# A first adaLN layer with half of one shift computed by columns on VectorE, loads in a fixed order, and sums of squares by tokens on ScalarE

## The chip, the cores and the metric

The kernel runs on one core of a Trainium2 chip. The metric is the device time of one execution in microseconds (us), the median of three runs. TensorE multiplies matrices, VectorE (DVE in the profile), ScalarE (ACT) and GpSimd (POOL) work element by element, and SyncE (SP) issues most of the transfers from the device's main memory (HBM).

## The reference: what is computed

Two layers over 1024 latent tokens and 256 context tokens of width 1024, all in fp32. Layer 0 mixes tokens by retention (4 heads), layer 1 by a short gated convolution; each is followed by a SwiGLU layer. Ahead of each mixer stands an RMS norm whose result is shifted and scaled (adaLN):

```python
def ada_params(cond, w, b):
    return jnp.split(jax.nn.silu(cond) @ w + b, 6, axis=-1)
def modulate(x, shift, scale):
    return x * (1 + scale) + shift
sh1, sc1, g1, sh2, sc2, g2 = ada_params(c, ada_w[i], ada_b[i])
ax = modulate(rms_norm(hx, norm_mix[i]), sh1, sc1)            # latent tokens
csh1, csc1, ... = ada_params(c_ctx, ada_w[i], ada_b[i])
ac = modulate(rms_norm(hc, norm_mix[i]), csh1, csc1)          # context tokens, layer 0
qx, kx, vx, gx = jnp.split(ax @ w_qkvg, [D, 2 * D, 4 * D], axis=-1)
kc, vc = jnp.split(ac @ w_qkvg[:, D:4 * D], [D], axis=-1)
```

Only the front of layer 0 matters here: the first shift (chunk 0 of the adaLN matrix, 1024 columns) and scale (chunk 1) for both conditions c and c_ctx, the norms of context and x, and the products of the context with the weights of k and v.

## The kernel before

Activations stand transposed: features on the 128 partitions (8 tiles, kt), tokens along the free axis. Every fp32 operand of a large product is split into a high and a low part of type fp32r (`split`, L132 on ScalarE and L133 on VectorE), and a product takes three passes of TensorE (`mm3`, L137 to L139).

The first adaLN is computed by `ada_both`, once for chunk 1 and once for chunk 0. For each half of 512 columns it loads four pieces of 512 KB (`ada_raw`, L169), multiplies them with the two columns Silu(c) and Silu(c_ctx) (`sc`) as the 2-column stationary operand (L237), copies the two result rows out of PSUM (L242), and turns them into columns by four small transposes (L247) into a bank `cps`; then it adds the bias (L252). The sixteen products of a half stand as 32 records in the trace, since each goes through TensorE in two passes. The later adaLN chunks are computed otherwise (`ada_next`, L210): VectorE multiplies a load of 128 transposed columns with a row Silu(c) that stands on all partitions (`c_row`, L192 and L193) and sums along the row in the same instruction.

The context tokens are loaded ahead of it (L489, on ScalarE's queue), squared on ScalarE (L261, L264), added on VectorE (L265), summed over features by products with ones (`rstd`, L270), and 1/rms is made on VectorE with small integer and float steps (L275, L143 to L155). 1/rms becomes diagonal matrices (L288), a product with ones spreads it over the partitions (`spread`, L296), and VectorE multiplies the context with scale and 1/rms (L512). With the shift added on the way (L527, L528) the context is the split operand `ac`.

Then `ctx_layer` multiplies the context with six blocks of weights, two of k and four of v. A block takes two loads of 1 MB (`ctx_load`, two pieces of 512 KB each, L483, from a pool of six such pieces), eight splits, and 96 records of L137 to L139 in two banks. Its two results are copied out at its end (L814) and stored. Between the products `unit_done` takes work from a queue of hooks: for each half of x (512 tokens) the squares (`sq`: ScalarE squares, GpSimd adds, L265), the diagonals (`diag`, with L270), the scaling (`mod`, L558 and L561), and the operands of the next products. x is loaded transposed, sixteen loads of 256 KB (`load_x`, L538).

The order of instructions on an engine, the SP queue with its loads included, is not that of the program: a list scheduler fills it with what is ready by its own estimate of time. That is how L483 loads stand ahead of the last four L169 loads, and the load of c_row ahead of x.

Of the kernel before, what the change touches and what calls it, by code (L numbers as in the profile page):

```python
# [52 lines left out]
def hybrid_kernel(ctx: ExitStack, tc: tile.TileContext, a: dict):  # L53
# [19 lines left out]
    def ttile():  # L73
        return tp.tile([P, 512], F32, tag="t", name="tt")
# [15 lines left out]
    def bank():  # L90
        return pp.tile([P, 512], F32, tag="p", name="ps")

    cols = const.tile([P, N_COLS], F32, name="cols")
    nc.sync.dma_start(cols, a["cols"])
    cc = const.tile([P, KT, 2], F32, name="cc")
    nc.sync.dma_start(cc, a["cc"])
    sc = const.tile([P, KT, 2], F32, name="sc")
# [66 lines left out]
    def ada_raw(b):  # L164

        out = []
        for half in range(2):
            r = raw()
            nc.sync.dma_start(r, a["ada_w"][b, :, half * 1024 : (half + 1) * 1024])  # L169
            out += [r[:, k * 256 : (k + 1) * 256] for k in range(4)]  # L170
        return out
# [19 lines left out]
    def ada_start():  # L191
        nc.sync.dma_start(c_row, a["c_row"].to_broadcast([P, D]))  # L192
        nc.scalar.activation(c_row, c_row, AF.Silu)  # L193
        ada_load(0)
        ada_load(1)
# [32 lines left out]

    def ada_both(i, chunk, mid=nothing):

        cps = bank()
        for half in range(2):
            ps = bank()
            for e in range(2):
                r = ada_raw(chunk * 4 + half * 2 + e)
                for kt in range(KT):
                    nc.tensor.matmul(  # L237
                        ps[:2, e * 256 : (e + 1) * 256], sc[:, kt], r[kt],
                        start=kt == 0, stop=kt == KT - 1,
                    )  # L240
            row = ttile()
            nc.scalar.copy(row[:2], ps[:2])  # L242
            if half == 0:
                mid()
# [5 lines left out]
        out = const.tile([P, KT, 2], F32, name=f"adab_{i}_{chunk}")  # L250
        o = C_ADAB + i * 48 + chunk * 8
        nc.vector.tensor_tensor(  # L252
            out, cps[:, : 2 * KT].rearrange("p (k v) -> p k v", v=2),
            cols[:, o : o + 8].unsqueeze(2).to_broadcast([P, KT, 2]), op=ALU.add,
        )
        return out


    def sq_add(acc, h, first, n=512, eng=nc.vector):
        if first:  # L260
            nc.scalar.activation(acc[:, :n], h, AF.Square)  # L261
        else:
            s = ttile()
            nc.scalar.activation(s[:, :n], h, AF.Square)  # L264
            eng.tensor_tensor(acc[:, :n], acc[:, :n], s[:, :n], op=ALU.add)  # L265

    def rstd(acc, nb, ps):

        for j in range(nb):
            nc.tensor.matmul(  # L270
                ps[:, j : j + 1], acc[:, j * P : (j + 1) * P], ones[:, 0:1],
                start=True, stop=True,
            )
        v = sm.tile([P, 8], F32, tag="rs_v", name="rs_v")
        nc.vector.tensor_scalar(  # L275
            v[:, :nb], ps[:, :nb], 1.0 / D, EPS, op0=ALU.mult, op1=ALU.add
        )
        y = sm.tile([P, 8], F32, tag="rs_y", name="rs_y")
        rsqrt(y[:, :nb], v[:, :nb], nb)
        return y  # L280

    def rstd_diag(acc, n):

        nb = n // P
        y = rstd(acc, nb, bank())
        dg = ttile()
        for j in range(nb):
            nc.vector.tensor_scalar(  # L288
                dg[:, j * P : (j + 1) * P], ident, y[:, j : j + 1], None, op0=ALU.mult
            )  # L290
        return dg

    def spread(dg, n):
# [183 lines left out]

    def piece(src):

        out = []  # L480
        for e in range(2):
            r = raw2()
            nc.sync.dma_start(r, src[:, e * 1024 : (e + 1) * 1024])  # L483
            out += [r[:, :512], r[:, 512:]]
        return out

    ct = [ttile() for _ in range(KT // 2)]
# [6 lines left out]
    box = {}  # L494
    s1 = ada_both(0, 1, lambda: box.update(dg=rstd_diag(acc, CTX)))
    to_scale(s1, cols[:, C_NMIX : C_NMIX + 8].unsqueeze(2).to_broadcast([P, KT, 2]))
# [4 lines left out]
    def ctx_load(n):  # L501
        if n < 2 * len(ctx_blocks):
            c_raws[n] = piece(ctx_blocks[n // 2][n % 2])

# [3 lines left out]

    def middle():
        rb = spread(box["dg"], CTX)  # L510
        for kt, h in enumerate(ch):
            nc.vector.scalar_tensor_tensor(  # L512
                h, h, s1[:, kt, 1:2], rb[:, :CTX], op0=ALU.mult, op1=ALU.mult
            )
        ctx_load(0)
        ctx_load(1)
        for kt in range(4):
            ctx_weight(0, kt)

    sh1 = ada_both(0, 0, middle)  # L520
    ac = {}
# [12 lines left out]
    xc = {n: {} for n in S_ALL}  # L534

    def load_x(tb):
        for kt in range(KT):
            nc.sync.dma_start(xt[kt, tb], a["xT"][kt, tb])  # L538

    def x_hooks(tb):  # L540
# [3 lines left out]
        def sq(k2):  # L544
            if k2 == 0:
                box["acc"] = ttile()
            for kt in (2 * k2, 2 * k2 + 1):
                sq_add(box["acc"], xt[kt, tb], kt == 0, TB, nc.gpsimd)

        def diag():  # L550
            box["dg"] = rstd_diag(box["acc"], TB)

# [1026 lines left out]
def _layout(i):  # L1579
# [13 lines left out]
    def paired(w):  # L1593
# [6 lines left out]
    arrays = {  # L1600
        "xT": i["x"][0].reshape(NTB, TB, KT, P).transpose(2, 0, 3, 1),
        "cxT": i["ctx"][0].reshape(CTX, KT // 2, 2, P).transpose(1, 3, 2, 0)
        .reshape(KT // 2, P, 2 * CTX),
# [4 lines left out]
        ),  # L1608
        "c_row": i["c"],
        "ada_w": i["ada_w"][0, :, : 2 * D].reshape(KT, P, -1, 256).transpose(2, 1, 0, 3)  # L1610
        .reshape(-1, P, KT * 256),
        "ada_t": np.concatenate([i["ada_w"][l, :, n * D : (n + 1) * D].T for l, n in ADA])
        .reshape(-1, P, D),
# [35 lines left out]
```

## Time and profile before

| | before |
|---|---|
| median of three runs | 2627.14 us (2623.88 to 2627.67) |
| profiled execution | 2628.3 us, its span 2626.4 us |
| TensorE busy (matmul) | 2565.5 us, 98% of the span |
| VectorE busy | 1889.3 us, 72% |
| ScalarE busy | 1235.6 us, 47% |
| GpSimd busy | 323.7 us, 12% |
| moved by DMA | 445.12 MB, mean 169 GB/s |

Times in rows are counted from the start of the span. A row of the timeline gives start, duration, engine, source line, operation, what it writes and reads, a count, and in brackets the idle time before it and what ended it. PE is TensorE, PEld its weight loads, SPq and ACTq are the sequencers that issue transfers. A row of a window gives the length, then the busy time of each engine with the number of instructions, the granted TensorE clock (1.00 is full speed), the DMA share and GB/s. A row of groups gives busy time and mean ns of one, then the idle time before them and what ended it.

### The profile page before, as it was taken

What the parts mean: (1) busy time and instruction counts of PE and PEld (TensorE: products, weight loads), DVE (VectorE), ACT (ScalarE), POOL (GpSimd) and SP (SyncE); (2) the same over time, 40 slices, a digit from 0 to 9 for tenths busy, and PEclk for the clock granted to TensorE, in tenths of its full rate; (3) what the DMA queues carried; (4) which work ended last, traced back from release to release, by engine and by line L of the source; (5) the groups of instructions that cost most, each with busy time, mean ns of one, the idle gap of its engine ahead of it and who ended that gap; (6) DMA issues with size and microseconds to landing.
All of it is one profiled execution on the core that took longest, in us unless ns stands there. A gap on an engine that the chain in (4) does not pass through costs nothing.

```text
span 2626.4 us, 33369 instructions
## 1 busy us (share of the span) xinstructions
PE 2565.5 (98%) x11508; PEld 2099.9 (80%) x11508; DVE 1889.3 (72%) x3333; ACT 1235.6 (47%) x2239; POOL 323.7 (12%) x370
## 2 busy tenths in 40 slices
PE   8999999999989999999999999999999999999998
PEld 4788888887777787888887888788777888887888
DVE  4886766767887867777776767777688666655766
ACT  4653232447776545433333545533366333333544
POOL 1100222002332102000001100200112000002100
PEclk9999999999999999999999999999999999999999
DMA  9546233764569957444556945432685333329733
GB/s 328 203 149 220 92 124 128 260 216 132 182 217 279 272 157 161 135 157 153 181 187 214 276 138 172 91 100 98 181 240 103 117 104 112 109 89 299 199 88 117
DMA packets 218985, 445.12 MB, mean 169 GB/s; under 512 B 23104, under 2 KB 52928, under 8 KB 218816
## 3 DMA queue, kind: packets, MB, share of 16 engines
q1 hardware_dynamic: 149232, 297.94, 35.4%
q0 software_dynamic: 32864, 79.19, 12.4%
q10 hardware_dynamic: 36720, 65.86, 6.7%
q8 instruction: 91, 1.49, 0.2%
q14 instruction: 78, 0.64, 0.1%
HBM read 320.74 MB, written 109.58 MB: 164 GB/s over the span
## 4 chain that ended last, share of the span: by engine, by line
PE 86%; DVE 6%; DMA 5%; issue 2%; ACT 1%; SPq 0%; DVEq 0%; ACTq 0%
PE ps L137 28%; PE ps L138 28%; PE ps L139 27%; DVE u L133 2%; PE ps L237 1%; DMA tt<-x_d 1%; DMA tt<-os_d 1%; DMA tt<-g_d 1%; DVE u L675 1%; PE ps L947 0%; DVE kh L634 0%; PE ps L296 0%; DMA raw<-in_w_g 0%; DVE tt L265 0%; PE ps L270 0%
## 5 line engine op out<-in xcount | busy, mean ns | idle before, releaser
L137 PE MATMUL ps<-u 128*128 128x512 f32 (+1 forms) x3492 | 1363.7, 391 | 17.9 <-DVE u L133 8.5
L138 PE MATMUL ps<-u 128*128 128x512 f32 (+1 forms) x3492 | 1356.7, 389 | 2.1 <-DVE u L133 1.9
L139 PE MATMUL ps<-u 128*128 128x512 f32 (+1 forms) x3492 | 1355.9, 389 | 0.0
L137 PEld LDWEIGHTS ps<-u 128*128 128x128 f32 x3492 | 659.1, 189 | 162.5 <-ACT u L132 10.0
L138 PEld LDWEIGHTS ps<-u 128*128 128x128 f32 x3492 | 659.7, 189 | 137.7 <-DVE u L133 4.7
L139 PEld LDWEIGHTS ps<-u 128*128 128x128 f32 x3492 | 659.4, 189 | 135.1 <-issue 0.7
L132 ACT CAST u<-raw 128x512 fp32r<-128x512 f32 x622 | 375.5, 619 | 379.9 <-PE ps L139 234.3
L133 DVE TENSOR_TENSOR u<-raw,u 128x512 fp32r<-128x512 f32 x622 | 434.8, 711 | 60.2 <-ACT u L132 59.4
L133 DVE TENSOR_TENSOR u<-tt,u 128x512 fp32r<-128x512 f32 x358 | 242.2, 700 | 123.4 <-ACT u L132 121.4
L132 ACT CAST u<-tt 128x512 fp32r<-128x512 f32 x358 | 211.9, 620 | 206.0 <-DMA tt<-x_d 102.4
L443 ACT COPY tt<-ps 128x512 f32<-128x512 f32 x192 | 112.6, 587 | 251.8 <-PE ps L139 244.5
L128 DVE SCALAR_TENSOR_TENSOR u<-raw,u 128x512 fp32r<-128x512 f32 x168 | 114.9, 688 | 76.6 <-ACT u L127 76.4
L127 ACT ACTIVATE u<-raw 128x512 fp32r<-128x512 f32 x168 | 105.1, 632 | 88.2 <-PE ps L139 75.8
L1263 POOL DMA_DIRECT2D x_d<-tt x52 | 28.3, 544 | 837.6 <-DVE tt L1276 774.2
L456 DVE TENSOR_TENSOR tt<-tt,ps 128x512 f32<-128x512 f32 x64 | 43.8, 684 | 80.3 <-PE ps L139 80.2
L675 DVE SCALAR_TENSOR_TENSOR u<-ps,u 128x512 fp32r<-128x512 f32 x128 | 84.9, 684 | 20.8 <-ACT u L674 20.7
L624 POOL TENSOR_TENSOR u<-t,u 128x512 fp32r<-128x512 f32 x40 | 55.3, 1386 | 279.3 <-ACT u L623 269.9
L450 DVE TENSOR_TENSOR tt<-tt,ps 128x512 f32<-128x512 f32 x64 | 44.0, 687 | 61.8 <-ACT tt L443 58.4
L674 ACT ACTIVATE u<-ps 128x512 fp32r<-128x512 f32 x128 | 74.2, 598 | 28.8 <-PE ps L139 26.8
L1146 DVE SCALAR_TENSOR_TENSOR t<-ps,ada,t 128x512 f32<-128x512 f32 x48 | 33.9, 747 | 53.3 <-PE ps L139 52.0
L210 DVE SCALAR_TENSOR_TENSOR raw<-raw,c_row 128x512 f32<-128x512 f32 x84 | 55.2, 686 | 20.1 <-DMA raw<-in_ada_t 20.0
L446 DVE TENSOR_TENSOR tt<-tt,ps 128x512 f32<-128x512 f32 x64 | 43.8, 684 | 23.7 <-PE ps L139 23.7
(162 smaller groups left out, 2054.5 us busy)
## 6 DMA issues: line engine op xcount, KB each, us to landing
tt<-x_d SPq DMA_DIRECT2D x182, 256.0 KB, 4.6
raw<-in_w SPq DMA_DIRECT2D x88, 512.0 KB, 4.1
raw<-in_w SPq DMA_DIRECT2D x88, 256.0 KB, 5.4
raw<-in_ada_t SPq DMA_DIRECT2D x42, 512.0 KB, 5.2
x_d<-tt ACTq DMA_DIRECT2D x78, 256.0 KB, 2.3
t<-in_ada_t SPq DMA_DIRECT2D x76, 256.0 KB, 6.3
raw<-in_w_v SPq DMA_DIRECT2D x36, 512.0 KB, 4.7
x_d<-tt POOLq DMA_DIRECT2D x52, 256.0 KB, 2.7
```

The lines of the kernel that those rows point to most:

```text
L127: nc.scalar.activation(dst_hi, src, AF.Copy, scale=-1.0)
L128: nc.vector.scalar_tensor_tensor(dst_lo, src, -1.0, dst_hi.bitcast(F32), op0=ALU.mult, op1=ALU.subtract)
L132: nc.scalar.copy(dst_hi, src)
L133: nc.vector.tensor_sub(dst_lo, src, dst_hi.bitcast(F32))
L137: nc.tensor.matmul(ps, w_hi, x_lo, start=first, stop=False, **kw)
L138: nc.tensor.matmul(ps, w_lo, x_hi, start=False, stop=False, **kw)
L139: nc.tensor.matmul(ps, w_hi, x_hi, start=False, stop=last, **kw)
L210: nc.vector.scalar_tensor_tensor(w[e], w[e], 1.0, c_row[:, k], op0=ALU.mult, op1=ALU.mult, accum_out=sums[:, e, ct : ct + 1],)
L443: nc.scalar.copy(m[p, n], ps)
L624: nc.gpsimd.tensor_sub(t[:, 1], v, t[:, 0].bitcast(F32))
L674: nc.scalar.activation(s[:, 0], st[d][m], AF.Copy, scale=f)
L675: nc.vector.scalar_tensor_tensor(s[:, 1], st[d][m], f, s[:, 0].bitcast(F32), op0=ALU.mult, op1=ALU.subtract,)
```

## The change

- The loads of the front and of the context products are pinned: `in_order` keeps them on the SP queue in the program's order, which is cc, four adaLN pieces of chunk 1, context, a column load, four of chunk 1, c_row, three column loads, four of chunk 0, and then context weights, x and rows of x. cols moves to ScalarE's queue.
- Half of chunk 0, the columns 512 to 1023, is no longer computed by TensorE. Four loads of 128 transposed columns (`ada_e`, 512 KB each) are multiplied on VectorE with the rows Silu(c) and Silu(c_ctx) and summed in the same instruction: 16 passes over 128x512, with c_ctx as soon as it can be, with c behind the scale. The row of c_ctx is loaded once (4 KB) and spread over the partitions by two products with ones; Silu is taken from PSUM. The row of c is loaded to all partitions as before, but earlier.
- The two half chunks of `ada_both` become `ada_half` with a `turn` that is called later.
- The sums of squares of x come from a second load of x, by tokens (`xr`, eight loads of 512 KB into the pool of split operands): ScalarE squares a tile of 128 tokens x 1024 features and sums along the row in the same instruction. The sums on GpSimd and the products of L270 for x fall away. The second half of x is loaded in the second block of the context products, the rows in the first.
- The hooks of x begin six empty steps later, and from the second block on two are taken at a time.

```diff
+    def in_order(dst, src):
+        tc.keep_in_program_order(nc.sync.dma_start(dst, src))
...
+    cx_row = raw()
+    nc.scalar.dma_start(cx_row[:1], a["cx_row"])
...
-    def ada_both(i, chunk, mid=nothing):
+    def ada_half(cps, chunk, half, between=nothing):
...
+    def early_load():
+        early_w.append(raw())
+        in_order(early_w[-1], a["ada_e"][len(early_w) - 1])
+
+    def early_sums(n, sums, v, out):
+        for e in range(2):
+            k = slice(e * 512, (e + 1) * 512)
+            nc.vector.scalar_tensor_tensor(
+                out, early_w[n][:, k], 1.0, (c_row, cx_row)[v][:, k], op0=ALU.mult, op1=ALU.mult,
+                accum_out=sums[:, e, n, v : v + 1],
+            )
...
+    for e in range(2):
+        k, ps = slice(e * 512, (e + 1) * 512), bank()
+        nc.tensor.matmul(ps, ones[:1], cx_row[:1, k], start=True, stop=True)
+        nc.scalar.activation(cx_row[:, k], ps, AF.Silu)
...
+    turn = ada_half(cps, 1, 0)
     ct = [ttile() for _ in range(KT // 2)]
     for t, src in zip(ct, a["cxT"]):
-        nc.scalar.dma_start(t, src)
+        in_order(t, src)
+    early_load()
...
+    early_sums(0, early, 1, junk)
+    dg = rstd_diag(acc, CTX)
+    turn()
+    turn = ada_half(cps, 1, 1)
+    in_order(c_row, a["c_row"].to_broadcast([P, D]))
+    nc.scalar.activation(c_row, c_row, AF.Silu)
+    for n in range(1, KT // 2):
+        early_load()
+        early_sums(n, early, 1, junk)
+    turn()
...
-    sh1 = ada_both(0, 0, middle)
+    cps = bank()
+    turn = ada_half(cps, 0, 0)
+    rb = spread(dg, CTX)
+    for kt, h in enumerate(ch):
+        nc.vector.scalar_tensor_tensor(
+            h, h, s1[:, kt, 1:2], rb[:, :CTX], op0=ALU.mult, op1=ALU.mult
+        )
+    for n in range(KT // 2):
+        early_sums(n, early, 0, junk)
...
+    ctx_load(0)
+    ctx_load(1)
+    turn()
...
+    def load_rows(tb):
+        for c in range(tb * 4, tb * 4 + 4):
+            xrows[c] = raw()
+            in_order(xrows[c], a["xr"][c])
...
         def sq(k2):
-            for kt in (2 * k2, 2 * k2 + 1):
-                sq_add(box["acc"], xt[kt, tb], kt == 0, TB, nc.gpsimd)
+            c = tb * 4 + k2
+            nc.scalar.activation(
+                xrows[c], xrows[c], AF.Square, accum_out=x_ss[:, c : c + 1]
+            )
...
         load_x(0)
         ctx_load(2)
-        load_x(1)
...
                     ctx_load(2 * b + 3 + kt // 4)
+                    if b == 0:
+                        load_rows(kt // 4)
+                    elif (b, kt) == (1, 0):
+                        load_x(1)
...
-                    unit_done(2 if b > 1 and kt % 4 == 1 else 1)
+                    unit_done(2 if b else 1)
...
-    hooks.extend(sq0 + mod0)
+    hooks.extend([nothing] * 6 + sq0 + mod0)
```

More of the change, by code (lines that the diff above doesn't have):

```diff
@@ L168, in ada_raw @@
             r = raw()
-            nc.sync.dma_start(r, a["ada_w"][b, :, half * 1024 : (half + 1) * 1024])
+            in_order(r, a["ada_w"][b, :, half * 1024 : (half + 1) * 1024])
             out += [r[:, k * 256 : (k + 1) * 256] for k in range(4)]
@@ L191, in ada_start @@
     def ada_start():
-        nc.sync.dma_start(c_row, a["c_row"].to_broadcast([P, D]))
-        nc.scalar.activation(c_row, c_row, AF.Silu)
         ada_load(0)
@@ L227, in urgent, with turn @@
         hooks.extendleft(reversed(work))
-    def ada_both(i, chunk, mid=nothing):
[L231 to L244, printed above, removed]
+    def ada_half(cps, chunk, half, between=nothing):
+        ps = bank()
+        raws = []
+        for e in range(2):
+            raws.append(ada_raw(chunk * 4 + half * 2 + e))
+            between()
+        for e, r in enumerate(raws):
+            for kt in range(KT):
+                nc.tensor.matmul(
+                    ps[:2, e * 256 : (e + 1) * 256], sc[:, kt], r[kt],
+                    start=kt == 0, stop=kt == KT - 1,
+                )
+        row = ttile()
+        nc.scalar.copy(row[:2], ps[:2])
+        def turn():
             for n in range(4):
@@ L249, in ada_both, with ada_bias @@
                 )
-        out = const.tile([P, KT, 2], F32, name=f"adab_{i}_{chunk}")
-        o = C_ADAB + i * 48 + chunk * 8
+        return turn
+    def ada_bias(out, src, chunk, c):
+        o = C_ADAB + chunk * 8
+        bias = cols[:, o + c.start : o + c.stop].unsqueeze(2)
         nc.vector.tensor_tensor(
-            out, cps[:, : 2 * KT].rearrange("p (k v) -> p k v", v=2),
-            cols[:, o : o + 8].unsqueeze(2).to_broadcast([P, KT, 2]), op=ALU.add,
-        )
-        return out
+            out[:, c], src, bias.to_broadcast([P, c.stop - c.start, 2]), op=ALU.add
+        )
+    early_w = []
+    def early_load():
[8 more added lines that the diff above has]
+            )
     def sq_add(acc, h, first, n=512, eng=nc.vector):
@@ L265, in sq_add, with root @@
             eng.tensor_tensor(acc[:, :n], acc[:, :n], s[:, :n], op=ALU.add)
+    def root(sums, nb):
+        v = sm.tile([P, 8], F32, tag="rs_v", name="rs_v")
+        nc.vector.tensor_scalar(
+            v[:, :nb], sums, 1.0 / D, EPS, op0=ALU.mult, op1=ALU.add
+        )
+        y = sm.tile([P, 8], F32, tag="rs_y", name="rs_y")
+        rsqrt(y[:, :nb], v[:, :nb], nb)
+        return y
     def rstd(acc, nb, ps):
@@ L273, in rstd, with diagonals @@
             )
[L274 to L285, printed above, removed]
+        return root(ps[:, :nb], nb)
+    def diagonals(y, n):
         dg = ttile()
-        for j in range(nb):
+        for j in range(n // P):
             nc.vector.tensor_scalar(
@@ L291, in rstd_diag @@
         return dg
+    def rstd_diag(acc, n):
+        return diagonals(rstd(acc, n // P, bank()), n)
     def spread(dg, n):
@@ L475, in hybrid_kernel, with piece @@
     h_d = spilled("h_d", KT, NTB)
-    def piece(src):
+    def piece(src, load=nc.sync.dma_start):
         out = []
@@ L482, in piece @@
             r = raw2()
-            nc.sync.dma_start(r, src[:, e * 1024 : (e + 1) * 1024])
+            load(r, src[:, e * 1024 : (e + 1) * 1024])
             out += [r[:, :512], r[:, 512:]]
         return out
+    for e in range(2):
+        k, ps = slice(e * 512, (e + 1) * 512), bank()
+        nc.tensor.matmul(ps, ones[:1], cx_row[:1, k], start=True, stop=True)
+        nc.scalar.activation(cx_row[:, k], ps, AF.Silu)
+    s1 = const.tile([P, KT, 2], F32, name="adab_0_1")
+    sh1 = const.tile([P, KT, 2], F32, name="adab_0_0")
+    early = sm.tile([P, 2, KT // 2, 2], F32, name="early", bufs=1)
+    junk = ttile()
+    cps = bank()
+    turn = ada_half(cps, 1, 0)
     ct = [ttile() for _ in range(KT // 2)]
     for t, src in zip(ct, a["cxT"]):
-        nc.scalar.dma_start(t, src)
+        in_order(t, src)
+    early_load()
     ch = [ct[kt // 2][:, (kt % 2) * CTX : (kt % 2 + 1) * CTX] for kt in range(KT)]
@@ L507, in ctx_weight @@
             c_ws[b, kt] = in_parts(c_raws[2 * b + kt // 4][kt % 4])
[L509 to L518, printed above, removed]
-    sh1 = ada_both(0, 0, middle)
+    cps = bank()
+    turn = ada_half(cps, 0, 0)
[3 more added lines that the diff above has]
+            h, h, s1[:, kt, 1:2], rb[:, :CTX], op0=ALU.mult, op1=ALU.mult
+        )
+    for n in range(KT // 2):
+        early_sums(n, early, 0, junk)
+    nc.vector.tensor_add(early[:, 0], early[:, 0], early[:, 1])
+    ada_bias(sh1, early[:, 0], 0, slice(KT // 2, KT))
+    ctx_load(0)
+    ctx_load(1)
+    turn()
+    ada_bias(sh1, cps[:, :KT].rearrange("p (k v) -> p k v", v=2), 0, slice(0, KT // 2))
+    for kt in range(4):
+        ctx_weight(0, kt)
     ac = {}
```

22 lines of the change are left out of this document (12 added, 10 removed).

## The prediction

> **What bounds the kernel now.** I read the page first, for the bound of the whole.
>
> ```profile
> span 2626.4 us, 33369 instructions
> PE 2565.5 (98%) x11508; PEld 2099.9 (80%) x11508; DVE 1889.3 (72%) x3333; ACT 1235.6 (47%) x2239; POOL 323.7 (12%) x370
> PE 86%; DVE 6%; DMA 5%; issue 2%; ACT 1%; SPq 0%; DVEq 0%; ACTq 0%
> ```
>
> TensorE sets the end. What the change can win is therefore time at the front, until TensorE begins the products of the first layer, and holes in the products just behind; from there on the same products follow one another, and I expect them only to shift. So I took the busy times by stage and the timeline of the first 44 us.
>
> ```profile
> core 0: us, PE busy (x) PEld busy (x) DVE busy (x) ACT busy (x) POOL busy (x), PEclk, DMA share, GB/s
> 9.00:43.40 34.40, 32.75 (x150) 12.99 (x148) 10.29 (x33) 6.30 (x14) 0.00 (x0) 1.00 1.03 402
> 43.40:58.00 14.60, 13.74 (x51) 10.48 (x52) 11.49 (x16) 14.60 (x31) 7.00 (x5) 0.88 0.70 238
> ```
> ```profile
> 1.66 16.08 SPq L169 DMA_DIRECT2D raw<-in_ada_w  x12
> 8.89 9.19 PE L237 MATMUL ps<-raw,sc 128*2 128x256 f32 x32 [8.89 <-DMA raw<-in_ada_w]
> 18.23 1.78 SPq L483 DMA_DIRECT2D raw<-in_w_kc  x4
> 19.14 7.93 PE L237 MATMUL ps<-raw,sc 128*2 128x256 f32 x36
> 20.22 4.14 SPq L169 DMA_DIRECT2D raw<-in_ada_w  x4
> 27.33 6.21 PE L237 MATMUL ps<-raw,sc 128*2 128x256 f32 x28
> 34.53 7.07 PE L237 MATMUL ps<-raw,sc 128*2 128x256 f32 x32
> 41.64 0.57 ACT L242 COPY tt<-ps 2x512 f32<-2x512 f32 x1 [7.49 <-PE ps L237]
> 43.48 0.86 PE L137 MATMUL ps<-u 128*128 128x512 f32 x2 [0.81 <-ACT u L527]
> ```
>
> The adaLN is four quarters of 32 records (32, 36, 28, 32 by the order in which they were put). TensorE waits 8.9 us for the first weights, is then busy nearly throughout, and the first context product starts at 43.5. The transfers are full as well (402 GB/s), but not all of that is needed: context weights (L483) pass the last four adaLN loads.
>
> Then the context products, 43.5 to 118:
>
> ```profile
> 43.40:47.10 3.70, 1.49 (x3) 0.96 (x4) 0.57 1.05 386
> 50.44 0.39 PE L139 MATMUL ps<-u 128*128 128x512 f32 x1
> 51.56 0.50 PE L137 MATMUL ps<-u 128*128 128x512 f32 x1 [0.73 <-DVE u L133]
> 62.92 0.95 PE L270 MATMUL ps<-ones,tt 128*128 128x1 f32 x8
> 71.80 0.39 PE L139 MATMUL ps<-u 128*128 128x512 f32 x1
> 74.09 1.50 PE L296 MATMUL ps<-tt,ones 128*128 128x512 f32 x2 [1.90 <-DVE tt L288]
> 75.60:78.20 2.60, 2.60 (x7) 2.02 (x7) 2.57 (x4) 1.79 (x3) 0.00 (x0) 0.53 1.04 401
> 84.43 1.27 ACT L814 COPY tt<-ps 128x512 f32<-128x512 f32 x2 [0.36 <-PE ps L139]
> 95.25 1.27 ACT L814 COPY tt<-ps 128x512 f32<-128x512 f32 x2 [0.20 <-PE ps L139]
> 118.02 1.27 ACT L814 COPY tt<-ps 128x512 f32<-128x512 f32 x2 [1.35 <-PE ps L139]
> ```
>
> (The first and the seventh row are windows; the column before the DMA share is the granted clock.) The copies of two undisturbed blocks stand 95.25 - 84.43 = 10.8 us apart, so six blocks need 64.9; they took 118.0 - 43.5 = 74.5. The 9.6 us over: a slow clock after the hole before 43.5, (1 - 0.57) x 3.7 = 1.6; a wait for VectorE, 51.56 - 50.44 less one step of 0.23, and a smaller one behind it, 1.1; the sums of squares on TensorE (L270), twice 0.8 = 1.6; the wait for the diagonals of 1/rms, 71.80 + 0.23 to 74.09 = 2.1; the spreading product itself, 1.5; the slow clock after it, (1 - 0.53) x 2.6 = 1.2. That is 9.1; 0.5 is scattered.
>
> Why VectorE is late at 51 and 74:
>
> ```profile
> L133 DVE TENSOR_TENSOR u<-raw,u 128x512 fp32r<-128x512 f32 x12 | 13.8, 1223 | 3.1 <-ACT u L132 3.1
> L265 POOL TENSOR_TENSOR tt<-tt 128x512 f32<-128x512 f32 x7 | 10.7, 1532 | 49.8 <-ACT tt L264 49.4
> 70.26 1.14 ACT L132 CAST u<-raw 128x512 fp32r<-128x512 f32 x2 [0.98 <-DMA raw<-in_w_v]
> 70.91 0.69 DVE L133 TENSOR_TENSOR u<-raw,u 128x512 fp32r<-128x512 f32 x1 [0.35 <-ACT u L132]
> ```
>
> From 49.5 to 63 the subtractions of the weight split take 1223 ns each, beside GpSimd's additions of squares; alone they take 0.69. And the steps of 1/rms stand on VectorE between subtractions that wait for a w_v load.
>
> **The change, part by part.**
>
> (1) Order of the loads. Eight loads of chunk 1 and four of chunk 0 stay on TensorE's way; four are replaced by four column loads of the same size. Time per 512 KB at the measured 402 GB/s: 524288 / 402e3 = 1.30 us, one U. First landing: the quickest context load took 3.0 us to land,
>
> ```profile
> DMA to landing us min/median/max: 3.0/5.4/9.0
> DMA packets 4574, 13.83 MB, mean 402 GB/s; under 512 B 772, under 2 KB 772, under 8 KB 4573
> ```
>
> at 256 KB; issued at 1.2 behind one small load and no longer beside the context loads, the first 512 KB land at 1.2 + 3.0 + 0.65 = 4.9 instead of 8.9. Pinned behind it: 3 adaLN loads, the context (2 U), one column load, 4 adaLN, c_row, 3 columns, 4 adaLN: 18 U, so the last adaLN load lands at 28.3.
>
> (2) TensorE until then. New: c_ctx is spread by ones, two fp32 products of 512 columns. The row at 74.09 has one such product at 1.50 on the slow clock, so 3 us, from about 3.3 (its row is small) to 6.5; it delays the first quarter by 1.6 but uses up the slow clock. Quarter 1: 6.5 to 14.0 (32 x 0.22 from the 7.07 row, plus the rest of the slow clock). Quarter 2 with the context's rms and transposes: to 22. Quarter 3 waits for loads: last one at 28.3, plus 8 records = 1.8, hence 30.1; if the hole near 22 slows the clock, as the hole before 43.5 did, up to 33. The tail from the last adaLN record to the first product was 43.48 - 41.6 = 1.9. TensorE alone would allow a start at 32 to 35.
>
> (3) VectorE until then. It gains 16 multiply-and-sum passes over 128x512 and the Silu of c_row (L193) moves forward on ScalarE.
>
> ```profile
> L210 DVE SCALAR_TENSOR_TENSOR raw<-raw,c_row x84: 679/686/694, 183.2 to 579.6; 128x512 f32<-128x512 f32 x84
> 34.20 3.22 DVE L512 SCALAR_TENSOR_TENSOR tt<-tt,adab,ps 128x256 f32<-128x256 f32 x8 [3.97 <-PE ps L296]
> 27.74 2.49 DVE L133 TENSOR_TENSOR u<-raw,u 128x512 fp32r<-128x512 f32 x4
> 33.47 0.70 PE L296 MATMUL ps<-tt,ones 128*128 128x256 f32 x2
> 46.13 1.04 ACT L193 ACTIVATE c_row<-c_row 128x1024 f32<-128x1024 f32 x1
> 54.35 1.15 ACT L264 ACTIVATE tt<-raw 128x512 f32<-128x512 f32 x2
> ```
>
> 16 x 0.69 = 11.0 us replace 7.07 on TensorE. The second column load lands at 4.9 + 12 U = 20.5; from there VectorE has six passes of c_ctx (4.1), eight of c (5.5), the eight context products (3.2), four splits (2.5) and some 0.7 of biases: 16.0, full until 36.5. The shift is ready when the passes are, about 34, and the splits may come behind it. I take the first context product at 35.5 instead of 43.5: 8.0 us. Bounds: 33, if TensorE alone decides and the clock stays up; 38.5, if the spreading of 1/rms is put behind quarter 3 (as it was before, the row at 33.47), which moves the eight context products to 34-37. What waits behind VectorE here is only the first product; the later blocks need 1.1 us of VectorE per 1.35 us of TensorE.
>
> (4) Squares of x from token rows on ScalarE with the sum in the instruction: two 128x512 squares, 1.15 the pair, become one of 1024 columns (the Silu of c_row, as wide, took 1.04), no GpSimd additions, no L270. Saved in the context products: 1.6 (L270) and 1.1 (VectorE's wait) outright. The wait of 2.1, the slow clock of 1.2 and 0.6 of the spreading product (0.9 at full clock) go only if the diagonals come in time.
>
> (5) The price of (4): eight more loads of 512 KB, pinned ahead of context weights. Behind the last adaLN load: 4 U of context weights (33.5), then x half 0 (4), weights (4), rows (4), weights (2), rows (4), weights (2), x half 1 (4), weights (2): 26 U. The weights of the fourth block land at 33.5 + 33.8 = 67.3, plus 1.3 for block 0's stores, 68.6. TensorE wants them at 35.5 + 1.6 + 3 x 10.8 = 69.5, and cast and subtraction need 1.3. So they come just in time, but steps of 1/rms that stand between these subtractions are late again: a wait of nothing up to 5 us (3 us and a slow clock of 1.2 as now, and a little). I take 2.
>
> **Sum.** Context products: 64.9 + slow clock 1.6 + spreading 0.9 + scattered 0.5 + wait 2.0 = 69.9, from 35.5 to 105.4, against 118.0: 12.6 us less. The profiled execution took 2628.3 (span 2626.4 and 1.9 around it), giving 2615.7; the median of the runs shown is 1.2 lower, so 2615. With the bounds of (3) and (5) the gain lies between 12.6 - 3.0 - 3.0 = 6.6 and 12.6 + 2.5 + 2.0 = 17.1, so the case's own range is 2610 to 2620.5.
>
> **Rivals.**
>
> A. The loads are slower than 402 GB/s once they are all needed. The profile has slow stretches:
>
> ```profile
> DMA packets 1587, 4.20 MB, mean 210 GB/s; under 512 B 171, under 2 KB 683, under 8 KB 1584
> SPq L483 <- DVE u L133: 45.0, 19, 8.9
> ```
>
> That is 50 to 70 us, and 45.0 us of the queue's waits there and later were for VectorE to free a buffer, not for the engines. If the true pace of the pinned run is 350 GB/s, U is 1.50: the last adaLN load lands at 31.9 (start near 37) and the fourth block's weights at 4.9 + 48 x 1.50 + 1.3 = 78.2 against 71 wanted, 8.5 us of waiting with the cast and subtraction, and a second slow clock. Without any wait the gain would be 14.6; less 1.5 of the start, 8.5 and 1.2 it is 3.4, time 2624. The Trainium skill, "DMA: Bandwidth & Descriptors", Specifications, gives an HBM limit of about 358 GB/s for a core; by that this would be the normal case, but the 34 us at 402 GB/s above stand against it. Chance 0.10.
>
> B. VectorE becomes the bound of the start: the passes of c stay behind the context products, which wait for a spreading product behind quarter 3. Then 33 + 0.7 + 3.2 + 5.5 + 0.4 + 0.5 = 43.3, no gain in front, and 9.6 - 5.0 = 4.6 in the context products: 2622.5. For it: that spreading product stood behind its quarter before (33.47). Against: the four splits at 27.74 were put ahead of the context products at 34.20, though they follow them in the program, so VectorE's order is filled by what is ready. Chance 0.10.
>
> C. Slower: the pinned queue stalls as a whole. One load without a free buffer holds all later ones, and the pace of 50 to 70 us (210 GB/s) lasts. The 26 U from 33.5 then take 13.6 MB / 210 = 65 us, the fourth block starts near 100 instead of 69.5: 30 lost against the 14.6, 2642. It turns slower than before when the stretch averages below 13.6 MB / 48 us = 285 GB/s. Against it: without GpSimd's additions VectorE frees the buffers at 0.69 each. Chance 0.07.
>
> D. The front is shorter, but the later stages do not shift with it, since a load or VectorE's adaLN passes are due there at a fixed time: 2625 to 2628. For it nothing but that VectorE is 72% busy; TensorE at 98% speaks against. Chance 0.05.
>
> **How the numbers follow.** Forecast 0.68, A 0.10, B 0.10, C 0.07, D 0.05. A measurement of this kernel tells about 0.2% (5.3 us) from no change, so faster means below 2622. The whole range of the forecast lies there, and about a third of A and B together: 0.75. Slower is C and a little of D, 0.08; the rest, 0.17, is no change. The range goes from 2608, the forecast's low end less 2 for the scatter between executions, to 2625, which holds A and B and leaves out C and D, 0.12, and some of the tails.
>
> **What would show it.** First context product (L137's successor) at 33 to 38.5, and no hole above 1 us in quarter 1 and 2; subtractions of the split near 0.69 all through the context products and no additions on GpSimd there; the sixth block's copy near 105; the fourth block not waiting for w_v. Wrong: a first product after 40 (B), waits for w_v above 5 us in blocks three to five (A, C), or a sixth copy near 105 with an end above 2622 (D).

## The result and the profile after

The changed kernel takes 2629.93 us (median of 20 runs, 2622.21 to 2638.25), the kernel before, run beside it, 2624.06 us (20 runs, 2620.06 to 2632.03): a ratio of 1.0017, 95% interval 1.0009 to 1.0025. The forecast was 12 us less than before; measured are 4 to 6 us more: 5.9 by these medians, and the profiled execution has a span of 2630.7 us, 4.3 more than before.

From the page of the kernel after, the span, the busy times and the shares of the chain that ended last:

```profile
span 2630.7 us, 33271 instructions
...
PE 2562.2 (97%) x11460; PEld 2098.1 (80%) x11460; DVE 1893.4 (72%) x3367; ACT 1236.4 (47%) x2240; POOL 301.9 (11%) x356
...
PE 86%; DVE 6%; DMA 5%; issue 2%; ACT 1%; POOL 0%; DVEq 0%; ACTq 0%; SPq 0%; POOLq 0%
```

TensorE works 3.3 us less and the span is 4.3 us longer, so TensorE stands idle some 7.6 us more than before. The whole page can't show where. (Lines have moved: the products `mm3` are now L143 to L145, the split is L138 on ScalarE and L139 on VectorE, the adaLN products L243, the copy of a result row L248, the column passes L276, squares and sums of the context L284, L287 and L288, spread L324, context products on VectorE L561, squares of rows L607, the copy of a block's result L875, its stores L880; all pinned loads L95.)

Windows of the kernel after, by stage (length, then busy time of PE, PEld, DVE, ACT and POOL with counts, granted clock, DMA share, GB/s), and then the waits of TensorE up to 140 us (total, times, longest):

```profile
6.60:16.20 9.60, 9.53 (x32) 3.12 (x32) 0.00 (x0) 0.32 (x2) 0.00 (x0) 1.00 1.04 406
16.20:21.10 4.90, 0.02 (x1) 0.02 (x1) 2.98 (x7) 3.02 (x10) 0.00 (x0) 0.73 1.02 408
22.50:31.00 8.50, 8.45 (x34) 2.92 (x33) 4.47 (x21) 0.02 (x1) 0.00 (x0) 0.84 1.03 410
39.00:47.80 8.80, 1.05 (x7) 0.56 (x6) 8.06 (x22) 1.13 (x3) 0.00 (x0) 0.69 0.72 251
47.80:122.90 75.10, 70.21 (x289) 56.98 (x290) 51.11 (x108) 53.75 (x101) 0.00 (x0) 0.95 0.81 284
66.10:69.60 3.50, 3.46 (x9) 2.72 (x9) 1.70 (x3) 3.50 (x7) 0.00 (x0) 0.52 1.00 384
```
```profile
PE ps L143 <- ACT u L580: 7.7, 1, 7.7
PE ps L303 <- DVE tt L288: 4.9, 1, 4.9
PE ps L143 <- DVE u L139: 4.9, 1, 4.9
```

There are three holes: 4.9 us behind the first quarter of the adaLN, 7.7 us ahead of the first context product, and 4.9 us ahead of the second block (61.26 to 66.14, with a clock of 0.52 for 3.5 us behind it). The transfers are as full as forecast through the front (406 to 410 GB/s).

**First hole: ScalarE's order.** Timeline of ScalarE in the kernel after:

```profile
16.19 0.57 ACT L248 COPY tt<-ps 2x512 f32<-2x512 f32 x1 [9.28 <-PE ps L243]
16.67 0.41 ACT L284 ACTIVATE tt<-tt 128x256 f32<-128x256 f32 x1
16.98 2.23 ACT L287 ACTIVATE tt<-tt 128x256 f32<-128x256 f32 x7
```

The copy of the first quarter's result row stands ahead of the squares of the context in ScalarE's list. It waits 9.28 us for TensorE to end the quarter; the squares, which need nothing of it, start behind it at 16.7. The sums on VectorE follow (17.42 to 21.03), and TensorE, whose next work is the sum of squares by ones (L303), waits until 21.08. The second quarter then runs on a clock of 0.84, in 8.4 us where 7.07 is full speed. In the kernel before, the squares stand ahead of that copy (timeline of ScalarE, before):

```profile
11.49 0.40 ACT L264 ACTIVATE tt<-tt 128x256 f32<-128x256 f32 x1
...
18.11 0.57 ACT L242 COPY tt<-ps 2x512 f32<-2x512 f32 x1 [6.22 <-PE ps L237]
```

**Second hole: VectorE's order.** Timeline of VectorE in the kernel after:

```profile
26.73 0.69 DVE L276 SCALAR_TENSOR_TENSOR tt<-raw 128x512 f32<-128x512 f32 x1
...
32.06 0.17 DVE L263 TENSOR_TENSOR adab<-ps,cols 128x16 f32<-128x16 f32 x1 [4.63 <-PE ps L253]
...
32.36 0.69 DVE L276 SCALAR_TENSOR_TENSOR tt<-raw 128x512 f32<-128x512 f32 x1
...
40.49 0.69 DVE L276 SCALAR_TENSOR_TENSOR tt<-raw,c_row 128x512 f32<-128x512 f32 x1
...
41.51 2.49 DVE L139 TENSOR_TENSOR u<-raw,u 128x512 fp32r<-128x512 f32 x4
43.92 3.22 DVE L561 SCALAR_TENSOR_TENSOR tt<-tt,adab,ps 128x256 f32<-128x256 f32 x8
```

Twelve of the sixteen column passes stand behind the bias of the scale (L263), which comes out of the second quarter, late by the first hole. VectorE is idle for 4.63 us; the last pass ends at 41.2, four splits follow, and only at 43.92 the eight context products, although the spread 1/rms was there at 39.65.

**Third hole: ScalarE again.** The second block's weights had landed by 48.8. Timeline of ScalarE in the kernel after:

```profile
60.67 0.59 ACT L875 COPY tt<-ps 128x512 f32<-128x512 f32 x1 [8.05 <-PE ps L145]
...
62.15 0.58 ACT L875 COPY tt<-ps 128x512 f32<-128x512 f32 x1 [0.89 <-PE ps L145]
...
63.62 1.06 ACT L607 ACTIVATE raw<-raw 128x1024 f32<-128x1024 f32 x1 [0.89 <-ACT tt L875]
...
64.67 2.16 ACT L138 CAST u<-raw 128x512 fp32r<-128x512 f32 x4
```

ScalarE sits idle for 8.05 us until the first block ends, since its two result copies stand ahead of the casts of the next block's weights. The casts begin at 64.67, the subtractions behind them at 65.30, and TensorE goes on at 66.14.

**Where the 4.7 us arise.** The start of the k-th record of `mm3` in each profiled execution, against before (10644 such records of 512 columns in all). A block of the context products has 48 of them (8 tiles, 2 groups of 128 tokens, 3 passes), not 96 as was said ahead; the "48th product triple" of an expectation below is the 48th record.

| k | before, us | after | what lies there |
|---|---|---|---|
| 0 | 43.5 | +4.3 | first product |
| 48 | 57.5 | +8.7 | second block |
| 96 | 69.3 | +9.4 | third block |
| 144 | 84.9 | +5.2 | fourth block (before waits for diagonals in the third) |
| 287 | 118.2 | +4.7 | last of the context products |
| 800 | 235.4 | +4.7 | |

From 118 us to 235 us the shift stays as it is. Between 780 and 1040 us profiled executions differ by several us whatever the kernel, so experiments are compared at k = 800 and by the ratio of their times.

### The profile page after: what moved, and what is told of

The parts are those of the page before. It is cut to its first block, busy times and chain, and to the rows that moved or that the text cites. A ratio compares the mean times of both kernels' runs of the same rounds, so it can differ in the third digit from the quotient of the medians.

```text
span 2630.7 us, 33271 instructions
## 1 busy us (share of the span) xinstructions
PE 2562.2 (97%) x11460; PEld 2098.1 (80%) x11460; DVE 1893.4 (72%) x3367; ACT 1236.4 (47%) x2240; POOL 301.9 (11%) x356
## 4 chain that ended last, share of the span: by engine, by line
PE 86%; DVE 6%; DMA 5%; issue 2%; ACT 1%; POOL 0%; DVEq 0%; ACTq 0%; SPq 0%; POOLq 0%
PE ps L143 28%; PE ps L144 28%; PE ps L145 28%; DVE u L139 1%; DMA tt<-os_d 1%; DMA tt<-g_d 1%; PE ps L243 1%; DVE u L736 1%; DVE tt L288 1%; DMA raw<-in_w 1%; DMA tt<-x_d 1%; PE ps L1011 0%; DMA raw<-in_w_g 0%; PE ps L303 0%; DVE kh L695 0%
## 5 line engine op out<-in xcount | busy, mean ns | idle before, releaser
L143 PE MATMUL ps<-u 128*128 128x512 f32 (+1 forms) x3492 | 1363.5, 391 | 28.7 <-DVE u L139 12.1
L145 PE MATMUL ps<-u 128*128 128x512 f32 (+1 forms) x3492 | 1355.1, 388 | 0.0
L143 PEld LDWEIGHTS ps<-u 128*128 128x128 f32 x3492 | 659.1, 189 | 172.3 <-issue 9.7
L145 PEld LDWEIGHTS ps<-u 128*128 128x128 f32 x3492 | 659.4, 189 | 134.8 <-issue 0.7
L138 ACT CAST u<-raw 128x512 fp32r<-128x512 f32 x622 | 375.8, 620 | 378.8 <-PE ps L145 229.6
L139 DVE TENSOR_TENSOR u<-raw,u 128x512 fp32r<-128x512 f32 x622 | 422.6, 693 | 70.6 <-ACT u L138 69.7
L139 DVE TENSOR_TENSOR u<-tt,u 128x512 fp32r<-128x512 f32 x358 | 242.4, 700 | 122.5 <-ACT u L138 119.6
L138 ACT CAST u<-tt 128x512 fp32r<-128x512 f32 x358 | 211.9, 620 | 206.8 <-DMA tt<-x_d 104.3
L134 DVE SCALAR_TENSOR_TENSOR u<-raw,u 128x512 fp32r<-128x512 f32 x168 | 114.9, 688 | 76.5 <-ACT u L133 76.3
L484 DVE TENSOR_TENSOR tt<-tt,ps 128x512 f32<-128x512 f32 x64 | 43.8, 684 | 81.4 <-PE ps L145 81.3
L736 DVE SCALAR_TENSOR_TENSOR u<-ps,u 128x512 fp32r<-128x512 f32 x128 | 84.9, 683 | 20.2 <-ACT u L735 20.1
L478 DVE TENSOR_TENSOR tt<-tt,ps 128x512 f32<-128x512 f32 x64 | 43.9, 686 | 60.8 <-ACT tt L471 60.2
L1045 POOL TENSOR_TENSOR raw<-tt,raw 128x512 f32<-128x512 f32 x16 | 24.3, 1516 | 396.5 <-DVE tt L474 285.1
```

What stands on the lines that cost most here:

```text
L134: nc.vector.scalar_tensor_tensor(dst_lo, src, -1.0, dst_hi.bitcast(F32), op0=ALU.mult, op1=ALU.subtract)
L138: nc.scalar.copy(dst_hi, src)
L139: nc.vector.tensor_sub(dst_lo, src, dst_hi.bitcast(F32))
L143: nc.tensor.matmul(ps, w_hi, x_lo, start=first, stop=False, **kw)
L145: nc.tensor.matmul(ps, w_hi, x_hi, start=False, stop=last, **kw)
L736: nc.vector.scalar_tensor_tensor(s[:, 1], st[d][m], f, s[:, 0].bitcast(F32), op0=ALU.mult, op1=ALU.subtract,)
```

## The experiments

Theory: the new work is as cheap as forecast, and what is lost is the order in which two engines hold it (row copy ahead of squares, bias ahead of passes, block copies ahead of casts). Rivals: the column passes are too much for VectorE; SP, which issues no load from 49 to 63 us, starves the second block; the new squares of rows cost more than they save.

**The row copy behind the squares.**

```diff
         row = ttile()
-        nc.scalar.copy(row[:2], ps[:2])
         def turn():
+            tc.keep_in_program_order(nc.scalar.copy(row[:2], ps[:2]))
```

> The changed kernel, but the copy of a quarter's two rows out of PSUM is put, on ScalarE's queue, behind the squares of the context (it is part of the later turn). Theory (the gain in front was lost because TensorE's second quarter waits for the context's squares, which stand behind that copy, and because VectorE's passes then stand behind the scale's bias): the hole of 4.9 us after quarter 1 goes, the scale is ready near 25.5 instead of 32, VectorE does its passes in the time it sat idle, and the first context product starts at 37 to 39 instead of 47.8; the time falls by about 9 us against the changed kernel, 3 to 4 below the kernel before. Rival (VectorE alone is the bound, its 16 passes fill the time whatever TensorE does): the first product at 45 or later.

Measured: 2619.48 us against 2624.67, ratio 0.9977 (0.9967 to 0.9987), span 2614.4. Timelines of ScalarE, VectorE and TensorE in this kernel:

```profile
11.16 0.42 ACT L284 ACTIVATE tt<-tt 128x256 f32<-128x256 f32 x1 [4.37 <-DMA tt<-in_cxT]
...
15.50 0.57 ACT L250 COPY tt<-ps 2x512 f32<-2x512 f32 x1 [1.62 <-PE ps L243]
```
```profile
22.11 0.69 DVE L276 SCALAR_TENSOR_TENSOR tt<-raw 128x512 f32<-128x512 f32 x1 [1.93 <-DMA raw<-in_ada_e]
...
31.73 0.69 DVE L276 SCALAR_TENSOR_TENSOR tt<-raw,c_row 128x512 f32<-128x512 f32 x1
...
33.95 3.21 DVE L561 SCALAR_TENSOR_TENSOR tt<-tt,adab,ps 128x256 f32<-128x256 f32 x8
```
```profile
6.29 9.18 PE L243 MATMUL ps<-raw,sc 128*2 128x256 f32 x32
15.58 0.61 PE L303 MATMUL ps<-ones,tt 128*128 128x1 f32 x4
...
16.53 7.07 PE L243 MATMUL ps<-raw,sc 128*2 128x256 f32 x32
...
25.96 7.07 PE L243 MATMUL ps<-raw,sc 128*2 128x256 f32 x32 [1.30 <-DMA raw<-in_ada_w]
32.96 0.70 PE L324 MATMUL ps<-tt,ones 128*128 128x256 f32 x2
...
37.83 1.19 PE L143 MATMUL ps<-u 128*128 128x512 f32 x2 [3.73 <-ACT u L580]
```

The copies of all three quarters move with this line. The first hole is gone, and with it the second: the bias comes at 25.66 between passes, fourteen of which run from 22.1 to 32.4 with nothing to wait for. The first context product starts at 37.8, 10.0 us earlier than after and 5.7 earlier than before. Of the 10.0, 6.0 are the earlier second quarter (16.53 against 22.54; the third keeps the same 6.0, 25.96 against 31.95), and 4.0 lie between spreading product and context products (43.92 - 38.95 = 5.0 after, 33.95 - 32.96 = 1.0 here). At k = 800 the shift is -5.8 us. One line in another place turns a loss into a gain; the third hole is still there (a wait of 4.8 us). The lists change elsewhere with it: on VectorE seven passes now stand ahead of the bias (four after) and two splits ahead of the context products (four after, 2.49 us), so a little over 1 us of the 4.0 is this order and not the earlier bias.

**The same without the column passes.** The loop of L276 is emptied and two small memsets on VectorE stand in for the sums; the upper half of the shift is then the bias alone.

> As the run with the late copy, and VectorE's 16 passes are left out (the upper half of the shift is its bias alone, so the output is not the reference's). What remains in front is TensorE and the loads: last adaLN load near 30, first context product at 33 to 35. The difference to the run with the late copy is what the passes cost: 3 to 4 us by the theory that they still end last there, nothing if loads or TensorE end last.

Measured: one time of 2622.67 us, span 2620.9; first product at 38.9, a miss: I had expected 33 to 35. Timeline of VectorE in this kernel:

```profile
25.60 0.17 DVE L168 SCALAR_TENSOR_TENSOR adab<-adab,cols 128x16 f32<-128x16 f32 x1
32.51 2.58 DVE L139 TENSOR_TENSOR u<-raw,u 128x512 fp32r<-128x512 f32 x4 [6.73 <-ACT u L138]
35.00 3.21 DVE L563 SCALAR_TENSOR_TENSOR tt<-tt,adab,ps 128x256 f32<-128x256 f32 x8
```

With 11 us of passes taken away VectorE stands idle for 6.73 us, then has four splits ahead of the context products instead of two, so this run alone doesn't price the passes. The run with the late copy does: there the context products start at 33.95, 0.3 us behind the end of the spreading product (32.96 + 0.70) that they need in any case. So once the order is right the passes cost next to nothing: they fill time in which VectorE would wait for TensorE's last quarter and for the weights. The rival "too much for VectorE" falls.

**The stores of the blocks on GpSimd's queue.**

```diff
-            nc.scalar.dma_start(v_d[b - 2][NCH + t], out)
+            nc.gpsimd.dma_start(v_d[b - 2][NCH + t], out)
...
-            nc.scalar.dma_start(
+            nc.gpsimd.dma_start(
```

The reason lies in SP's timeline and the waits of its queue in the kernel after:

```profile
44.41 4.75 SPq L95 DMA_DIRECT2D raw<-in_xr  x4
63.06 0.82 SPq L95 DMA_DIRECT2D raw<-in_w_v  x2
```
```profile
SPq L95 <- DMA k_d<-tt: 21.4, 4, 13.8
```

SP waits 13.8 us with a load of w_v for a *store* of the first block, issued by ScalarE, to land; in the trace the store lands at 63.00 and the load is issued at 63.06. The two have no data in common. In the trace the store and the load carry the same semaphore for "landed", and SP waits for that one directly ahead of the load: both queues use the same few in turn, and a load takes one only when the transfer that had it before is done.

> The changed kernel with the stores of the context's k and v issued from GpSimd's queue instead of ScalarE's. Theory (a load on SP waits for the completion of a store from ScalarE's queue, since the two queues take turns on the same few completion semaphores, and the store waits for the end of its block): the stretch of 14 us in which SP issues nothing (49 to 63) goes, the w_v load behind it is issued before 56; block 2 (the second) still starts near 65, since its casts stand behind the copies of block 1 on ScalarE. The time falls by 0 to 3 us against the changed kernel. Rival (SP waits there for a buffer of the weight pool): the stretch stays.

Measured: 2627.37 us against 2624.67, ratio 1.001 (1.000 to 1.002), shift at k = 800 +2.4. SP's timeline and waits in this kernel:

```profile
44.74 2.09 SPq L95 DMA_DIRECT2D raw<-in_xr  x4
52.75 1.53 SPq L95 DMA_DIRECT2D raw<-in_w_v  x2
```
```profile
SPq L95 <- DVE u L139: 41.8, 16, 7.0
```

The wait for the store is gone, and the next load leaves 10.3 us earlier, but what follows waits for VectorE to free buffers. TensorE's wait at the second block falls from 4.9 to 3.1 us. The stall is real and costs about 2.3 us of the 4.7; it isn't what makes the third hole.

**The old squares of x under the new front.** The sums of squares of x are made as before (from the transposed x, additions on GpSimd, sums by products with ones), with the x loads and hooks where they were; the front stays as changed.

```diff
-            c = tb * 4 + k2
-            nc.scalar.activation(
-                xrows[c], xrows[c], AF.Square, accum_out=x_ss[:, c : c + 1]
-            )
+            if k2 == 0:
+                box["acc"] = ttile()
+            for kt in (2 * k2, 2 * k2 + 1):
+                sq_add(box["acc"], xt[kt, tb], kt == 0, TB, nc.gpsimd)
```

> The changed kernel with the sums of squares of x as before (ScalarE squares, GpSimd adds, L270 on TensorE, x loaded in two halves one behind the other, no rows, the old hooks): the new front alone. Theory (front loses about 4.3 us, the new squares win almost nothing net): first product again near 47.8, subtractions of the split at 1.2 us beside GpSimd, and the end within 3 us of the changed kernel. Rival (the new squares are what costs): the end 4 us or more below the changed kernel.

Measured: 2631.52 us against 2624.67, ratio 1.0029 (1.0019 to 1.0039), first product at 47.3, shift at k = 800 +5.3. The front alone carries the loss; the row squares, as they stand in the changed kernel, give 0.6 us at k = 800 (about 3 us by the ratios, 1.0029 and 1.0017, whose intervals overlap). The third hole isn't in this kernel: the shift is +3.8 at k = 0 and at k = 48, since four casts of the second block stand ahead of the copies in ScalarE's list (TensorE waits 3.1 us later, in the middle of that block). Timeline of ScalarE in this kernel:

```profile
56.19 2.17 ACT L138 CAST u<-raw 128x512 fp32r<-128x512 f32 x4
60.53 1.28 ACT L874 COPY tt<-ps 128x512 f32<-128x512 f32 x2 [2.17 <-PE ps L145]
```

**The block copies behind the next casts.**

```diff
         out = ttile()
-        nc.scalar.copy(out, ps)
+        tc.keep_in_program_order(nc.scalar.copy(out, ps))
```

> The changed kernel with one edit in the context products: the copies of a block's results are pinned on ScalarE behind the casts of the next block's weights, as in the program. Theory (5.8 us of TensorE at the start of the second block, and a slow clock behind it, are lost because those casts stand behind the copies, which wait for the end of the block): no hole above 2 us at the first record of block 2, the 48th product triple at 59 to 61 instead of 66.1; the end of the context products about 5 us earlier, the time about that of the kernel before. Rival (the weights of block 2 are simply not there yet, loads being late): the hole stays.

Measured: 2622.47 us against 2626.14, ratio 0.9986 (0.9973 to 0.9998). Timeline of ScalarE in this kernel:

```profile
61.89 2.17 ACT L138 CAST u<-raw 128x512 fp32r<-128x512 f32 x4
63.97 0.58 ACT L875 COPY tt<-ps 128x512 f32<-128x512 f32 x1
64.44 0.62 ACT L138 CAST u<-raw 128x512 fp32r<-128x512 f32 x1
...
65.44 0.59 ACT L875 COPY tt<-ps 128x512 f32<-128x512 f32 x1 [0.37 <-ACT u L138]
```

TensorE doesn't wait at the second block any more; the shift goes from +2.9 at k = 48 to -2.8 at k = 800, though the first product is nearly as late as after (47.1 against 47.8). This move alone is worth 7.5 us at k = 800, 0.7 of it ahead of the first product.

**Both moves.** The row copy in `turn` and the pinned block copies, together.

> Both orders mended: the row copy behind the context's squares and the block copies behind the next casts. First context product at 37.5 to 38.5, the second block without a hole above 2 us, the time 3 to 6 us below the run with the late copy alone, near 2615: the forecast's own number. Rival (the loads then end last, since rows and weights come too late for an earlier start): a hole for w_v loads of 3 us or more in blocks 2 to 4 and no gain over the late copy alone.

Measured: 2611.71 us against 2626.14, ratio 0.9950 (0.9937 to 0.9962); first product at 37.8, shift at k = 800 -10.8. This version beats both kernels.

**Both moves, and the stores on GpSimd's queue.**

> As the run before, and the stores from GpSimd's queue. If SP's waits for store completions still cost TensorE anything, 1 to 3 us less; if the loads are early enough without it, the same within 1 us.

Measured: 2611.60 us, ratio 0.9950 (0.9936 to 0.9964), shift -10.6. Nothing more is gained: with the copies behind the casts SP is early enough.

**The late row copy with the old squares of x.**

> The mended front (row copy behind the context's squares) with the squares of x as before. Theory (the new squares win little, since what they save on VectorE and TensorE they pay in the second block's hole): first product at 37 to 39, VectorE's subtractions at 1.2 us beside GpSimd, the time 0 to 3 us above the run with the late copy. Rival (the new squares win what was forecast, 5 us): 4 us or more above it.

Measured: 2621.23 us against 2626.14, ratio 0.9983 (0.9972 to 0.9994), shift -4.3. Against -5.8 with the row squares this leaves them 1.5 us, still far from the 4.6 of the prediction.

**What the row squares are worth when nothing else is in the way.** Three kernels side by side: both moves with the old squares, both moves again, and the kernel before with the block copies pinned (the same edit as above, in its own line L814).

> The kernel with both moves (row copy of a quarter behind the context's squares, block result copies behind the next block's casts), but with the squares of x as in the kernel before (columns, additions on GpSimd, sums on TensorE). Theory (the row squares are worth what the prediction's part 4 said, and it only showed badly beside the other holes): first product near 37.8 as with both moves, L139 again at 0.9 us or more in the first blocks, context products 2.5 to 5 us longer, time 2614 to 2617 against 2611.7. Rival (the row squares give nothing, since their eight loads and their steps on VectorE and ScalarE take what they save): within 1 us of 2611.7.

> The kernel with both moves again, on the same chip and beside the same runs of the kernel before as e9_mended_old_squares: ratio 0.994 to 0.996, span 2607 to 2611.

> The kernel before with the block result copies alone put behind the next block's casts. Theory (those copies became late only because the change shifted the work on ScalarE's queue, and before they cost 0.2 to 1.4 us a block): within 2 us of the kernel before, ratio 0.9992 to 1.0008. Rival (the copies were a cost of their own in the kernel before too, so that half of the mended kernel's gain has nothing to do with the change): 4 us or more faster, ratio below 0.9985.

Measured against 2625.3 us: old squares 2623.84 us, ratio 0.9989 (0.9978 to 0.9999); both moves again 2612.58 us, 0.9958 (0.9944 to 0.9971); before with pinned copies 2623.60 us, 0.9993 (0.9982 to 1.0003). At k = 800 the shifts are -4.0, -10.8 and -1.3. The windows from the first to the last context product, first of the kernel with both moves, then of the one with the old squares, and after them VectorE's subtractions from 37 to 120 us (groups; the same order):

```profile
37.80:107.40 69.60, 68.22 (x289) 55.35 (x290) 51.47 (x110) 53.45 (x103) 0.00 (x0) 0.98 0.95 345
```
```profile
38.00:114.30 76.30, 73.06 (x306) 58.47 (x307) 62.98 (x106) 52.93 (x100) 21.43 (x14) 0.95 0.76 255
```
```profile
L139 DVE TENSOR_TENSOR u<-raw,u 128x512 fp32r<-128x512 f32 x64 | 40.0, 687 | 9.6 <-ACT u L138 9.5
```
```profile
L139 DVE TENSOR_TENSOR u<-raw,u 128x512 fp32r<-128x512 f32 x64 | 53.2, 884 | 4.8 <-ACT u L138 4.8
```

The front is the same in both; the context products take 69.6 us with the row squares and 76.3 without. So they are worth 6.7 us here, 1.5 with the third hole open and 0.6 with all three: a late block hides what they save. This is the worth of the whole part, since the edit also puts the loads and hooks of x back: 2.2 of the 6.7 are a shorter wait inside the second block (0.9 us against 3.1). My own expectation of 2.5 to 5 us was low. And the pinned copies are not a gain of their own: without the change they bring 1.3 us, beside the old squares nothing (-4.3 and -4.0), and beside the row squares 5.0 to 7.5. They belong to the change: with squares of 1.05 us each on the queue where the casts stand, the list puts those casts behind the copies, and with the old squares it doesn't.

## Why the prediction was wrong

Sizes first, order second: nearly every size held, and the order didn't.

**(1) Order of the loads: right but for the start.** The pace was 403 to 410 GB/s, as taken. The first weights landed at 6.5, not 4.9, which costs next to nothing (0.35 us) as long as c_ctx is spread until 6.3. With the late copy TensorE waits once for adaLN loads, 1.30 us, at 25.96.

**(2) TensorE until then: the step that failed.** "Quarter 2 with the context's rms and transposes: to 22" holds only if the rms is in time. I worked out when TensorE and the loads are ready and didn't ask what stands ahead of the squares on ScalarE; the step had been harmless before because the squares were done at 11.9 and stood ahead of the copy at 18.11. Quarter 2 ended at 31 instead of 22: 7.4 us later than in the kernel with the late copy, where it ends at 23.6 (6.0 of them are left at quarter 3, which waits there for a load). A second term was mis-sized: for quarter 1 I took 32 times 0.22 and "the rest of the slow clock", 7.5 us, and let the spreading of c_ctx use up the slow clock. It took 9.5 us (9.18 with the late copy), as in the row of before that the prediction itself shows (8.89, 9.19): the spreading did not use up the slow clock.

**(3) VectorE until then: sizes right, argument wrong.** Sixteen passes took 0.69 each (11.0, and 0.08 for reading each sum). With the late copy VectorE is full from 22.1 to 37.1, forecast were 20.5 to 36.5, and the first product at 37.8 lies in the forecast's bounds of 33 to 38.5, at the end that I gave for a spreading of 1/rms behind quarter 3 (32.96); that is where it stood. In the kernel as changed it started at 47.8. What I held against rival B, that "VectorE's order is filled by what is ready", is what fell: the order is a list made ahead of the run by estimates, and on the chip VectorE stood idle for 4.63 us with twelve ready passes behind one bias. The Trainium skill, "TensorE: Matmul & The Clock Gate", Part 1, says that ScalarE and VectorE take their instructions strictly first in, first out; all three holes agree (waits of 9.28, 4.63 and 8.05 us, in the first from about 11.4 on, with ready work behind the waiting instruction).

**(4) Squares by rows: right, and hidden.** No additions on GpSimd, subtractions at 0.69 instead of 1.22 us, no products of L270. In the mended kernel the context products take 69.6 us; the sum said 69.9. That it agrees so closely is luck: the 2 us for the fourth block didn't come, and instead the first two blocks took 13.2 and 12.1 us where an undisturbed one takes 10.8.

**(5) The price: wrong cause.** I took 2 us for the fourth block's weights coming just in time. They came in time. The price was the second block, 4.9 us of waiting and (1 - 0.52) x 3.5 = 1.7 of slow clock, from casts behind the first block's copies. The prediction named what is queued on SP and VectorE, not on ScalarE.

**Sum.** Forecast -8.0 in front and -4.6 in the context products. Measured after: +4.3 and +0.4. Measured with both moves: -5.7 and -5.1, together -10.8 in the trace, and -12.7 and -14.4 us by the medians of its two comparisons. So the kernel that the forecast describes differs from the changed one in the place of two copies. That its medians reach the forecast's 12 us is in part luck: 10.8 us lie in the stretches of the sum, 2.3 less in front and 0.5 more behind, and the rest lies behind 235 us, where the forecast had no term.

**Rivals.** A: no, the loads kept at 403 to 410 GB/s until the last adaLN load was in. B: nearest in place, VectorE bounds the start at 43.9, but not by its reason; the passes stood ahead of the context products, not behind. Its time, 2622.5, was too low, since nothing in it made TensorE wait. C: a stall of the whole pinned queue did come, 13.8 us long, but from a store and not for want of a buffer, and it cost 2.3 us. D: no, the shift at 118 us is that at 235.

**What stays open.** Why the list puts the row copy ahead of the context's squares, and the block copies ahead of the casts as soon as the row squares are there, wasn't looked into; only that it does, and what it costs. Nor is it settled why executions differ between 780 and 1040 us: there the shift of the kernel with both moves goes from -13.3 to -17.2 in one profiled execution and from -14.5 to -20.3 in the other, and that of the kernel before with pinned copies from -2.8 to -8.3, so a part of every difference of spans is not the edit's. This is why no verdict above rests on the spans.

## What to carry to other kernels

When work is moved, write down for every engine it touches what stands directly ahead of it in that engine's list and which wait that carries, ScalarE's small copies and VectorE's small biases included: a 0.6 us copy that waited 9.28 us for TensorE let the squares behind it start at 16.7 instead of 11.2. If a scheduler makes the lists, pin the small instruction that waits (the copy of a result) behind the ready work of the next stage. And before a part of a change is dropped because it gives nothing, close the holes beside it: the row squares gave 0.6, 1.5 or 6.7 us by what else was late.

## What the runs showed of the hardware that was not expected

- A load can wait for a store of another queue that shares no data with it: 13.8 us on SP, until the store of k_d had landed; with the stores on GpSimd's queue the wait was gone. In the trace both carry the same semaphore for the landing.
- After 3.75 us of products of one partition TensorE was still slow. It worked from 2.41 to 6.16 in the kernel with the late copy (four records of the spreading of c_ctx) and still ran the first ten adaLN records 0.43 us apart until 10.5, and then 0.216. In the kernel before, with no product ahead of them, the slow records last as long: 8.89 to 13.11. In the windows of the kernel after, 10 records take 4.0 us and the next 24 take 5.6, with a granted clock of 1.00 in both, so this column doesn't show the slow start:

```profile
6.60:10.60 4.00, 3.98 (x10) 1.25 (x11) 0.00 (x0) 0.30 (x1) 0.00 (x0) 1.00 1.04 405
10.60:16.20 5.60, 5.55 (x24) 1.87 (x21) 0.00 (x0) 0.01 (x1) 0.00 (x0) 1.00 1.04 407
```

  The Trainium skill, "TensorE: Matmul & The Clock Gate", Part 1, says that the clock comes up after one busy window of about 3.4 us that runs freely, so, as an estimate from it, at most two windows or 6.8 us after the work begins. Counted from 6.29 the 4.2 us agree with it; counted from 2.41 the 8.1 us don't. No run here separates the reason (one partition, or the gap of 0.13 us).
- A subtraction of 128x512 on VectorE takes 687 ns on average with GpSimd idle and 884 ns over the same 64 with 14 GpSimd instructions beside them.
